# One turn of values moved two products on, spare raw rows and VectorE halves for the first weights, queries and keys stored with their halves side by side

## The chip, the cores and the metric

The kernel runs on one core of a Trainium2 chip. Five engines of that core matter here: TensorE (PE in the profile, with PEld for its weight loads), VectorE (DVE), ScalarE (ACT), GpSimd (POOL) and SyncE (SP), whose queue issues all DMA transfers of this kernel. The metric is the device time of one execution in microseconds (us), as a median of several runs; lower is better.

## The reference

One layer of a hybrid decoder on 2048 tokens of 1024 channels, all in float32:

```python
a = _rmsnorm(h, g_pre_mix[l])
u = jnp.einsum("bsd,dc->bsc", a, w_in[l])          # value | gate | q | k | v, 512 columns each
conv_out = _conformer_conv(c_val, c_gate, ...)     # value * sigmoid(gate), 31 taps, LayerNorm, silu
attn_out = _stick_breaking(q, k, v)                # 8 heads of 64, causal, no softmax
attn_out = _rmsnorm(attn_out, attn_norm_g[l])
y = jnp.einsum("bsc,cd->bsd", concat(conv_out, attn_out), w_out[l])
h = h + _rmsnorm(y, g_post_mix[l])
f_in = _rmsnorm(h, g_pre_ffn[l])
f = jnp.einsum("bsf,fd->bsd", silu(f_in @ w_gate[l]) * (f_in @ w_up[l]), w_down[l])   # 2816 wide
h = h + _rmsnorm(f, g_post_ffn[l])
```

In the stick-breaking attention a query reads only earlier keys, with weight sigmoid(z) times the product of (1 - sigmoid(z)) of all keys between.

## The kernel before

**Precision.** Every float32 operand of a product is split into a rounded half H and a rest L, and a product is made of three passes: L·H, H·H and H·L (`dense`, L606 to L615). A weight's H is a ScalarE copy (L565), its L a GpSimd subtraction (L569) that is also written to DRAM (L571), so that later groups load it (L567) and subtract nothing. `load_w` (L557) does this for one weight tile of 128x1024; its raw rows have two buffers, H and L three each, and `Weights` (L585) loads two products ahead.

**Groups.** The 2048 tokens go in four groups of 512 (`g` from 0 to 3). For each group `inproj` (L766) makes 20 products of 24 matmuls each, four times in the order gate, value ("val"), query, key, value of the attention ("v"), one for each block of 128 columns. Each product fills one PSUM bank of the pool `mm`, which has two banks, taken in turn (`bank`, L527); a product can start only when the engine that reads the bank's product of two turns ago has read it. What reads it: ScalarE's sigmoid for the gate (`sg`, L781), VectorE's multiplication for the value (`glu`, L786), ScalarE and VectorE for the halves of query and key (`split`, L601), ScalarE's copy for v (`vs`, L789).

**The turn of values.** Attention reads differences of neighbouring v rows, transposed. GpSimd makes the differences (`step`, L792 to L794). TensorE transposes them into a bank of the same pool (`vps`, four transposes, L799), and ScalarE and VectorE split that in two parts (`vt`, L804), which SP stores (L805). This is the function `later`; it is called after the next product, the gate of the next block (L776). At the last block of a group it follows at the end.

**Queries and keys in DRAM.** A query or key product holds two heads of 64 rows. Its H and L are stored as four pieces of 64x512 (128 KB each, L817 and L818), by head and half. When a head of a group begins (`begin`, L897), its queries are loaded four times 64x512 into QH and QL, each half of the rows twice; `fetch` (L906) loads one 128x512 piece of keys, H over L.

**Order.** `inproj`, the attention (`attn`), the 31 taps of the convolution (`taps`, VectorE, L833 and L837) and the sums of the feed-forward weights (`sums`, GpSimd, L1201) are recorded one beside the other. Then a planner (`Graph`, L243) takes all recorded instructions, models their durations (`cost`), the waits between them and the DMAs, and fixes the order on each engine by list scheduling with backward priorities in several rounds (`arrange`, L456; `in_order`, L469). It takes overlaps of tiles from `box` (L162). An engine then executes its instructions in that order, so that an instruction that waits holds up all behind it. SP's queue too is in that order, and the built program makes nearly every DMA wait until the one eight places ahead of it has landed. From some 1100 us on the feed-forward products run, to the end.

Of the kernel before, what the change touches and what calls it, by code (L numbers as in the profile page):

```python
# [10 lines left out]
F32 = mybir.dt.float32  # L11
F32R = mybir.dt.float32r
BF16 = mybir.dt.bfloat16
AF = mybir.ActivationFunctionType
ALU = mybir.AluOpType
# [4 lines left out]
P = 128  # L20
S = 2048
D = 1024
# [139 lines left out]
def box(a):  # L162
# [7 lines left out]
    p0, f0 = divmod(int(a.bass_ap.offset), row // size)  # L170
    cur = [(f0, f0 + 1)]
# [9 lines left out]
    return p0, p0 + dims[0][1], [(x * size, y * size) for x, y in cur]  # L181
# [311 lines left out]
def layer_kernel(ctx: ExitStack, tc: tile.TileContext, x, xT, g_pre_mix, w_in, conv_w, conv_b, ln_g, ln_b,  # L493
# [62 lines left out]

    def load_w(w):  # L557
# [5 lines left out]
        raw = wp.tile([P, D], F32, tag="raw", name="raw")  # L563
# [5 lines left out]
        nc.gpsimd.tensor_tensor(L, raw, H.bitcast(F32), ALU.subtract)  # L569
# [98 lines left out]
    for g in range(NG):  # L668
        for h in range(NH):
            qd[h, g] = dp.tile([2, DH, G], F32R, name=f"qd{h}_{g}")  # L670
            kd[h, g] = dp.tile([P, G], F32R, name=f"kd{h}_{g}")
        for p in range(CB):
            vd[p, g] = dp.tile([P, 2, G], F32R, name=f"vd{p}_{g}")
# [92 lines left out]
    def inproj(g, order):  # L766
# [5 lines left out]
        later = None  # L772
        for kind, c in order:
            ps = bank("inps")
            dense([ps], *wts.next(), aH, aL)
            if later is not None:  # L776
                later()
                later = None
# [8 lines left out]
            elif kind == "v":  # L787
# [8 lines left out]
                def later(c=c, vs=step):  # L796
# [9 lines left out]
                    done.add(("v", g, c))  # L806
            else:
# [3 lines left out]
                for h in range(2):  # L811
                    hp = slice(h * DH, (h + 1) * DH)
                    if kind == "q":
                        dsts = (qd[2 * c + h, g][0], qd[2 * c + h, g][1])
                    else:
                        dsts = (kd[2 * c + h, g][0:DH, :], kd[2 * c + h, g][DH:P, :])
                    nc.sync.dma_start(dsts[0].bitcast(F32), H[hp, :].bitcast(F32))  # L817
                    nc.sync.dma_start(dsts[1].bitcast(F32), L[hp, :].bitcast(F32))  # L818
# [3 lines left out]
        if later is not None:  # L822
            later()
# [68 lines left out]
    def attn(g):  # L892
# [4 lines left out]
        def begin(h):  # L897
            QH = ap.tile([P, G], F32R, tag="QH", name="QH")
            QL = ap.tile([P, G], F32R, tag="QL", name="QL")
            for i in range(2):  # L900
                hp = slice(i * DH, (i + 1) * DH)
                nc.sync.dma_start(QH[hp, :].bitcast(F32), qd[h, g][0].bitcast(F32))
                nc.sync.dma_start(QL[hp, :].bitcast(F32), qd[h, g][1].bitcast(F32))
# [897 lines left out]
```

## Time and profile before

| | us |
|---|---|
| median of three runs | 2370.36 (2368.6 to 2370.89) |
| the profiled execution itself | 2367.53 |
| its span, first to last instruction | 2365.4 |

Busy time of the other engines in the span, from the same page: DVE 1711.8 us (72%), ACT 1179.5 us (50%), POOL 1241.8 us (52%). The DMA queue moves 656.68 MB. The granted TensorE clock is 0.998 of full speed on average.

Of the views that the prediction uses, the **waits** view lists for each engine which instruction it was idle for and by whom it was released (total us, times, longest). The **timeline** lists an engine's instructions: start us, duration us, engine, line, operation, output and inputs, and in brackets the idle time before it. A matmul's duration is modelled and overlaps the next one; the distance of two starts is what a matmul costs. The **windows** view gives busy us (and number) of PE, PEld, DVE, ACT and POOL in stretches of the span, then clock, DMA share and GB/s.

### The profile page before, as it was taken

What the parts mean: (1) busy time and instruction counts of PE and PEld (TensorE: products, weight loads), DVE (VectorE), ACT (ScalarE), POOL (GpSimd) and SP (SyncE); (2) the same over time, 40 slices, a digit from 0 to 9 for tenths busy, and PEclk for the clock granted to TensorE, in tenths of its full rate; (3) what the DMA queues carried; (4) which work ended last, traced back from release to release, by engine and by line L of the source; (5) the groups of instructions that cost most, each with busy time, mean ns of one, the idle gap of its engine ahead of it and who ended that gap; (6) DMA issues with size and microseconds to landing.
All of it is one profiled execution on the core that took longest, in us unless ns stands there. A gap on an engine that the chain in (4) does not pass through costs nothing.

```text
span 2365.4 us, 33884 instructions
## 1 busy us (share of the span) xinstructions
PE 2330.6 (99%) x11156; PEld 1927.4 (81%) x11156; DVE 1711.8 (72%) x2121; ACT 1179.5 (50%) x2102; POOL 1241.8 (52%) x1050
## 2 busy tenths in 40 slices
PE   7999999999999999999999999999999999999998
PEld 5878888788888878888888888888888888888886
DVE  5896899899997799946741257888666664557556
ACT  5456555574664455455654554334223335455543
POOL 5473346621652333446510158769976445478556
PEclk9999999999999999999999999999999999999999
DMA  9988877998789799987899768999998667668665
GB/s 329 294 274 309 260 261 236 314 300 266 248 306 301 263 321 321 338 282 269 272 320 318 262 229 308 302 313 332 362 345 291 200 236 232 196 199 297 226 194 178
DMA packets 283791, 656.68 MB, mean 278 GB/s; under 512 B 34912, under 2 KB 35424, under 8 KB 283616
## 3 DMA queue, kind: packets, MB, share of 16 engines
q1 hardware_dynamic: 283616, 654.52, 81.8%
q8 instruction: 88, 1.44, 0.2%
q14 instruction: 87, 0.71, 0.1%
HBM read 460.40 MB, written 193.99 MB: 277 GB/s over the span
## 4 chain that ended last, share of the span: by engine, by line
PE 91%; DVE 4%; DMA 2%; POOL 1%; issue 1%; ACT 1%; SPq 1%; POOLq 0%; DVEq 0%; ACTq 0%
PE b L1117 22%; PE dps L1117 17%; PE c L1117 10%; PE inps L611 5%; PE inps L613 5%; PE inps L615 5%; PE at L946 4%; PE p L1117 3%; PE ops L1053 2%; PE ops L1054 2%; PE ops L1055 2%; PE z L921 2%; PE z L920 2%; PE o L951 2%; PE o L952 2%
## 5 line engine op out<-in xcount | busy, mean ns | idle before, releaser
L837 DVE SCALAR_TENSOR_TENSOR cv<-glu,cw,cv 128x512 f32<-128x512 f32 x464 | 348.0, 750 | 9.0
L1407 POOL TENSOR_TENSOR wL<-raw,wH 128x512 fp32r<-128x512 f32 x176 | 266.4, 1538 | 147.4 <-ACT wH L1406 136.2
L1637 DVE TENSOR_TENSOR xL__20102<-t__20104,xH__20101 128x512 fp32r<-128x512 f32 x154 | 200.0, 1300 | 160.5 <-ACT xH__20101 L1636 156.0
L1635 POOL TENSOR_TENSOR xL__20100<-t__20103,xH__20099 128x512 fp32r<-128x512 f32 x154 | 208.0, 1353 | 157.7 <-ACT xH__20099 L1634 149.3
L604 DVE TENSOR_TENSOR TL<-at,TH 128x512 fp32r<-128x512 f32 (+1 forms) x320 | 189.8, 601 | 125.2 <-ACT TH L603 112.4
L611 PE MATMUL inps<-xH,wL 128*128 128x512 f32 x640 | 257.5, 403 | 7.6 <-ACT sg L781 6.5
L613 PE MATMUL inps<-xH,wH 128*128 128x512 f32 x640 | 255.0, 399 | 0.0
L615 PE MATMUL inps<-xL,wH 128*128 128x512 f32 x640 | 254.4, 399 | 0.0
L928 DVE TENSOR_TENSOR_SCAN om<-z,om,one 128x512 f32<-128x512 f32 x168 | 213.5, 1276 | 45.5 <-ACT z L923 45.0
L1117 PE MATMUL dps<-xH__20099,xL__20102 128*128 128x512 f32 x616 | 239.8, 389 | 0.2 <-DVE xL__20102 L1637 0.2
L1117 PE MATMUL dps<-xH__20099,xH__20101 128*128 128x512 f32 x616 | 239.5, 389 | 0.0
L1117 PE MATMUL dps<-xL__20100,xH__20101 128*128 128x512 f32 x616 | 239.1, 389 | 0.0
L565 ACT ACTIVATE wH<-raw 128x1024 fp32r<-128x1024 f32 x156 | 165.2, 1060 | 144.1 <-PE inps L615 87.7
L923 ACT ACTIVATE z<-z 128x512 f32<-128x512 f32 (+2 forms) x320 | 167.2, 528 | 97.6 <-PE z L921 92.8
L603 ACT ACTIVATE TH<-at 128x512 fp32r<-128x512 f32 (+1 forms) x320 | 169.1, 534 | 82.0 <-PE at L946 70.9
L569 POOL TENSOR_TENSOR wL<-raw,wH 128x1024 fp32r<-128x1024 f32 x50 | 120.6, 2413 | 151.3 <-ACT wH L565 103.2
L1634 ACT ACTIVATE xH__20099<-t__20103 128x512 fp32r<-128x512 f32 x154 | 97.2, 631 | 205.5 <-POOL xL__20100 L1635 165.6
L946 PE MATMUL at<-idr,om 128*128 128x128 f32 x1088 | 185.5, 272 | 0.6 <-DVE om L928 0.4
L1406 ACT ACTIVATE wH<-raw 128x512 fp32r<-128x512 f32 x176 | 101.6, 624 | 167.8 <-PE b L1117 65.5
L946 PEld LDWEIGHTS at<-idr,om 128*128 128x128 f32 x1088 | 137.8, 140 | 37.3 <-DVE om L928 1.6
L1201 POOL TENSOR_TENSOR sum<-sum 128x512 f32<-128x512 f32 x88 | 117.5, 1335 | 66.3 <-issue 22.1
L611 PEld LDWEIGHTS inps<-xH,wL 128*128 128x128 f32 x640 | 121.0, 189 | 30.8 <-ACT sg L781 7.6
(295 smaller groups left out, 6029.8 us busy)
## 6 DMA issues: line engine op xcount, KB each, us to landing
wL<-wL SPq DMA_DIRECT2D x156, 512.0 KB, 5.3
raw<-in_w_in_dram SPq DMA_DIRECT2D x80, 512.0 KB, 5.7
t__20104<-u SPq DMA_DIRECT2D x154, 256.0 KB, 3.0
c<-c SPq DMA_DIRECT2D x88, 256.0 KB, 4.9
t__20103<-wd SPq DMA_DIRECT2D x88, 256.0 KB, 2.7
K<-kd SPq DMA_DIRECT2D x80, 256.0 KB, 4.5
V<-vd SPq DMA_DIRECT2D x80, 256.0 KB, 4.6
u<-accf SPq DMA_DIRECT2D x22, 768.0 KB, 6.7
```

What stands on the lines that cost most here:

```text
L603: nc.scalar.activation(H, ps, AF.Copy)
L604: nc.vector.tensor_tensor(L, ps, H.bitcast(F32), ALU.subtract)
L611: nc.tensor.matmul(ps, WL[:, kc], aH[t](k), start=k == 0, stop=False)
L613: nc.tensor.matmul(ps, WH[:, kc], aH[t](k), start=False, stop=False)
L615: nc.tensor.matmul(ps, WH[:, kc], aL[t](k), start=False, stop=k == KT - 1)
L837: nc.vector.scalar_tensor_tensor(to, gl[c][:, k:k + G], cw[:, c, k:k + 1], a, ALU.mult, ALU.add)
L928: nc.vector.tensor_tensor_scan(r, zr, one.to_broadcast([P, w]), hd_["prev"][j], ALU.mult, ALU.bypass)
L946: nc.tensor.transpose(pt[:, j * P:(j + 1) * P], u["A"][j][:, b * P:(b + 1) * P], id32)
L1117: return nc.tensor.matmul(ps, a, b, skip_group_check=True, **flags)
L1407: nc.gpsimd.tensor_tensor(l, t, f32(h), sub)
L1635: nc.gpsimd.tensor_tensor(WL, w, f32(WH), sub)
L1637: nc.vector.tensor_tensor(UL, t, f32(UH), sub)
```

## The change

Five edits:

1. `later` becomes `turn` and waits in a list; the turn of v runs after the second product behind it (value of the next block), not the first (gate).
2. Every second weight tile of the first group takes its raw rows from a new tile `raw2` (`spare`), made in the buffers that the mixed outputs use later; so up to four raw tiles more can be in flight.
3. The L halves of the first four weight tiles are subtracted by VectorE, not GpSimd.
4. Queries and keys lie in DRAM as 128 x 2 x 512, H and L of a row side by side. A product is stored by two transfers of 128x512 (256 KB), not four of 64x512; a head's queries are loaded by two transfers of 64x1024, not four of 64x512, with the two copies on every other partition. That makes 64 stores and 64 loads less. A key tile then holds H and L in alternate rows, as the query tile holds its two copies.
5. `box` is told how to cover steps between partitions and rows that are part of a DRAM row.

```diff
+    halves_ = []
+
+    def spare():
+
+        if not halves_:
+            t = cm.tile([P, 2, D], F32, tag="big", name="raw2", bufs=2)
+            halves_.extend([t[:, 1, :], t[:, 0, :]])
+        return halves_.pop()
...
-        raw = wp.tile([P, D], F32, tag="raw", name="raw")
+        raw = spare() if src is w_in and key not in kept and len(kept) % 2 else wp.tile([P, D], F32, tag="raw", name="raw")
...
-        nc.gpsimd.tensor_tensor(L, raw, H.bitcast(F32), ALU.subtract)
+        (nc.vector if len(kept) < 4 else nc.gpsimd).tensor_tensor(L, raw, H.bitcast(F32), ALU.subtract)
...
-        for h in range(NH):
-            qd[h, g] = dp.tile([2, DH, G], F32R, name=f"qd{h}_{g}")
-            kd[h, g] = dp.tile([P, G], F32R, name=f"kd{h}_{g}")
         for p in range(CB):
+            qd[p, g] = dp.tile([P, 2, G], F32R, name=f"qd{p}_{g}")
+            kd[p, g] = dp.tile([P, 2, G], F32R, name=f"kd{p}_{g}")
...
-        later = None
-        for kind, c in order:
+        behind = []
+        for n, (kind, c) in enumerate(order):
             ps = bank("inps")
             dense([ps], *wts.next(), aH, aL)
-            if later is not None:
-                later()
-                later = None
+            if behind and behind[0][0] <= n:
+                behind.pop(0)[1]()
...
-                def later(c=c, vs=step):
+                def turn(c=c, vs=step):
...
+                behind.append((n + 2, turn))
...
-                for h in range(2):
-                    hp = slice(h * DH, (h + 1) * DH)
...
-                    nc.sync.dma_start(dsts[0].bitcast(F32), H[hp, :].bitcast(F32))
-                    nc.sync.dma_start(dsts[1].bitcast(F32), L[hp, :].bitcast(F32))
+                to = (qd if kind == "q" else kd)[c, g]
+                for a, t in enumerate((H, L)):
+                    nc.sync.dma_start(to[:, a, :].bitcast(F32), t.bitcast(F32))
...
-            QH = ap.tile([P, G], F32R, tag="QH", name="QH")
-            QL = ap.tile([P, G], F32R, tag="QL", name="QL")
+            Q = ap.tile([P, 2, G], F32R, tag="Q", name="Q")
+            half = qd[h // 2, g][h % 2 * DH:(h % 2 + 1) * DH]
             for i in range(2):
-                hp = slice(i * DH, (i + 1) * DH)
-                nc.sync.dma_start(QH[hp, :].bitcast(F32), qd[h, g][0].bitcast(F32))
-                nc.sync.dma_start(QL[hp, :].bitcast(F32), qd[h, g][1].bitcast(F32))
+                nc.sync.dma_start(Q[slice(i, P, 2), :, :].bitcast(F32), half.bitcast(F32))
...
-            nc.sync.dma_start(K.bitcast(F32), kd[h, c].bitcast(F32))
+            half = kd[h // 2, c][h % 2 * DH:(h % 2 + 1) * DH].rearrange("p a t -> (p a) t")
+            nc.sync.dma_start(K.bitcast(F32), half.bitcast(F32))
```

Because the planner orders everything anew, instructions move on all engines. Three places follow, each as the built programs have it (line, operation, output and inputs, shape of the output, and how many in a row).

On ScalarE, around the first turn of the first group: before, from the copy of the first key to the second gate's sigmoid `sg`.

```order
L603 ACTIVATE qkH<-inps 128x512
L724 ACTIVATE xcol<-xcol,gpm 128x512 x6
L789 ACTIVATE vs<-inps 128x512
L724 ACTIVATE xcol<-xcol,gpm 128x512 x2
L565 ACTIVATE wH<-raw 128x1024 x2
L603 ACTIVATE vt<-vps 128x4x64 x2
L781 ACTIVATE sg<-inps 128x512
```

The same stretch of ScalarE in the changed kernel, from the H half of the eighth weight tile on:

```order
L578 ACTIVATE wH<-raw_450 128x1024
L736 ACTIVATE xcol<-xcol,gpm 128x512 x2
L800 ACTIVATE vs<-inps 128x512
L736 ACTIVATE xcol<-xcol,gpm 128x512
L578 ACTIVATE wH<-raw 128x1024
L736 ACTIVATE xcol<-xcol,gpm 128x512
L792 ACTIVATE sg<-inps 128x512
L578 ACTIVATE wH<-raw_741 128x1024
L616 ACTIVATE vt<-vps 128x4x64
L736 ACTIVATE xcol<-xcol,gpm 128x512
L616 ACTIVATE vt<-vps 128x4x64
```

The sigmoid of the second gate stood behind both `vt` copies and now stands ahead of them.

On VectorE at the same place, before: the taps of the first conv block (`cv`, the last one writes `acc`), the query and key halves `qkL`, and the two `vt` parts; the second block's multiplication `glu_140` comes only after nine more rows, of the attention and of the next query product.

```order
L604 TENSOR_TENSOR qkL<-inps,qkH 128x512
L837 SCALAR_TENSOR_TENSOR cv<-glu_138,cw,cv 128x512 x7
L604 TENSOR_TENSOR qkL<-inps,qkH 128x512
L837 SCALAR_TENSOR_TENSOR cv<-glu_138,cw,cv 128x512 x16
L837 SCALAR_TENSOR_TENSOR acc<-glu_138,cw,cv 128x512
L604 TENSOR_TENSOR vt<-vps,vt 128x4x64 x2
```

And in the changed kernel:

```order
L617 TENSOR_TENSOR qkL<-inps,qkH 128x512
L845 SCALAR_TENSOR_TENSOR cv<-glu_138,cw,cv 128x512 x7
L617 TENSOR_TENSOR qkL<-inps,qkH 128x512
L845 SCALAR_TENSOR_TENSOR cv<-glu_138,cw,cv 128x512 x15
L845 SCALAR_TENSOR_TENSOR acc<-glu_138,cw,cv 128x512
L797 TENSOR_TENSOR glu_140<-inps,sg 128x512
L841 TENSOR_SCALAR cv<-glu_140,cw,small_121 128x512
L617 TENSOR_TENSOR vt<-vps,vt 128x4x64
L845 SCALAR_TENSOR_TENSOR cv<-glu_140,cw,cv 128x512 x2
L617 TENSOR_TENSOR vt<-vps,vt 128x4x64
```

The second block's multiplication now follows the last tap directly, ahead of both `vt` parts.

On VectorE at the start of the program, before: the scaled token rows `xrow`, the halves `xL` of the first group's input, the first multiplication and the first taps.

```order
L648 CAST idr<-ident 128x128
L697 TENSOR_SCALAR xrow<-xrow,rs 128x1024 x4
L624 SCALAR_TENSOR_TENSOR xL<-tps,gpm,xH 128x512 x8
L786 TENSOR_TENSOR glu_138<-inps,sg 128x512
L833 TENSOR_SCALAR cv<-glu_138,cw,small_121 128x512
```

And in the changed kernel:

```order
L661 CAST idr<-ident 128x128
L709 TENSOR_SCALAR xrow<-xrow,rs 128x1024 x3
L582 TENSOR_TENSOR wL<-raw,wH 128x1024
L709 TENSOR_SCALAR xrow<-xrow,rs 128x1024
L582 TENSOR_TENSOR wL<-raw_311,wH 128x1024
L582 TENSOR_TENSOR wL<-raw,wH 128x1024
L637 SCALAR_TENSOR_TENSOR xL<-tps,gpm,xH 128x512 x8
L582 TENSOR_TENSOR wL<-raw_311,wH 128x1024
L797 TENSOR_TENSOR glu_138<-inps,sg 128x512
```

One of the four weight halves stands ahead of the fourth token row, two ahead of all `xL`, and one behind them. ScalarE likewise makes three weight copies `wH`, where it made two, ahead of its eight `xH`.

More of the change, by code (lines that the diff above doesn't have):

```diff
@@ L170, in box @@
     p0, f0 = divmod(int(a.bass_ap.offset), row // size)
+    step, rows = dims[0]
+    if step * size % row:
+        return p0, p0 + -(-step * size * rows // row) + (f0 > 0), [(0, row)]
+    rows = (rows - 1) * (step * size // row) + 1
     cur = [(f0, f0 + 1)]
@@ L180, in box @@
             cur = [(x + step * k, y + step * k) for k in range(n) for x, y in low]
-    return p0, p0 + dims[0][1], [(x * size, y * size) for x, y in cur]
+    return p0, p0 + rows, [(x * size, y * size) for x, y in cur]
 def meet(a, b):
@@ L810, in inproj @@
                 split(ps, H, L)
-                for h in range(2):
-                    hp = slice(h * DH, (h + 1) * DH)
[L813 to L816, printed above, removed]
-                    nc.sync.dma_start(dsts[0].bitcast(F32), H[hp, :].bitcast(F32))
-                    nc.sync.dma_start(dsts[1].bitcast(F32), L[hp, :].bitcast(F32))
+                to = (qd if kind == "q" else kd)[c, g]
+                for a, t in enumerate((H, L)):
+                    nc.sync.dma_start(to[:, a, :].bitcast(F32), t.bitcast(F32))
             if kind != "v":
@@ L821, in inproj @@
             yield 1
-        if later is not None:
-            later()
+        for _, turn in behind:
+            turn()
     conv = {}
@@ L897, in begin @@
         def begin(h):
-            QH = ap.tile([P, G], F32R, tag="QH", name="QH")
-            QL = ap.tile([P, G], F32R, tag="QL", name="QL")
+            Q = ap.tile([P, 2, G], F32R, tag="Q", name="Q")
+            half = qd[h // 2, g][h % 2 * DH:(h % 2 + 1) * DH]
             for i in range(2):
-                hp = slice(i * DH, (i + 1) * DH)
-                nc.sync.dma_start(QH[hp, :].bitcast(F32), qd[h, g][0].bitcast(F32))
-                nc.sync.dma_start(QL[hp, :].bitcast(F32), qd[h, g][1].bitcast(F32))
-            return dict(QH=QH, QL=QL, prev=[lower[:, 0:1]] * TT, o=None)
+                nc.sync.dma_start(Q[slice(i, P, 2), :, :].bitcast(F32), half.bitcast(F32))
+            return dict(Q=Q, prev=[lower[:, 0:1]] * TT, o=None)
         def fetch(h, c):
@@ L919, in scores @@
             js = slice(j * P, (j + 1) * P)
-            nc.tensor.matmul(z[:, 0:w], hd_["QL"][:, js], K[:, 0:w], start=True, stop=False)
-            nc.tensor.matmul(z[:, 0:w], hd_["QH"][:, js], K[:, 0:w], start=False, stop=True)
+            nc.tensor.matmul(z[:, 0:w], hd_["Q"][:, 1, js], K[:, 0:w], start=True, stop=False)
+            nc.tensor.matmul(z[:, 0:w], hd_["Q"][:, 0, js], K[:, 0:w], start=False, stop=True)
             om = ap.tile([P, G], F32, tag="om", name="om", bufs=NOM)
```

## The prediction

> **What bounds the kernel now.** I read the page's busy times first, then TensorE's own waits, then the windows by stage, then the timeline where a wait is long.
>
> ```profile
> span 2365.4 us, 33884 instructions
> PE 2330.6 (99%) x11156; PEld 1927.4 (81%) x11156; DVE 1711.8 (72%) x2121; ACT 1179.5 (50%) x2102; POOL 1241.8 (52%) x1050
> ...
> PE tps L621 <- DVE xrow L697: 8.9, 4, 7.2
> PE inps L611 <- ACT sg L781: 6.5, 4, 4.1
> PE po L984 <- DVE ot L976: 3.7, 2, 2.8
> ...
> PE inps L611 <- POOL wL L569: 1.1, 1, 1.1
> ...
> 50.00:60.00 10.00, 4.80 (x18) 3.41 (x17) 6.48 (x10) 2.31 (x4) 5.12 (x6) 0.83 1.01 320
> 60.00:200.00 140.00, 136.76 (x710) 114.67 (x709) 128.71 (x192) 72.85 (x140) 78.81 (x71) 1.00 0.90 299
> 200.00:1100.00 900.00, 893.75 (x4576) 738.75 (x4575) 775.72 (x1055) 510.92 (x915) 380.31 (x371) 1.00 0.84 284
> 1100.00:2300.00 1200.00, 1199.91 (x5448) 992.97 (x5447) 729.28 (x782) 537.54 (x950) 703.34 (x521) 1.00 0.81 273
> ```
>
> TensorE is busy 99% of the span, and from 1100 to 2300 us it idles 0.09 us in 1200 (1200.00 - 1199.91). The change takes no matmul away, so it can win only what TensorE waits for before 1100 us: 5.2 us between 50 and 60 us, 3.24 (140.00 - 136.76) and 6.25 (900.00 - 893.75) after that, and something of the start, whose 8.9 us are mostly the wait for the first tokens. No line of TensorE's waits names a DMA. The one large piece is at 51 us.
>
> ```profile
> 51.02 0.39 PE L615 MATMUL inps<-xL,wH 128*128 128x512 f32 x1
> 52.46 0.66 PE L799 MATMUL vps<-idr,step 128*128 128x128 f32 x4 [1.05 <-POOL step L793]
> 57.26 0.80 PE L611 MATMUL inps<-xH,wL 128*128 128x512 f32 x1 [4.14 <-ACT sg L781]
> 57.85 0.63 PE L613 MATMUL inps<-xH,wH 128*128 128x512 f32 x1
> 58.28 0.63 PE L615 MATMUL inps<-xL,wH 128*128 128x512 f32 x1
> ...
> 60.27 0.40 PE L613 MATMUL inps<-xH,wH 128*128 128x512 f32 x1
> 60.50 0.40 PE L615 MATMUL inps<-xL,wH 128*128 128x512 f32 x1
> ...
> 90.11 0.60 PE L799 MATMUL vps<-idr,step 128*128 128x128 f32 x4
> 90.47 0.49 PE L615 MATMUL inps<-xL,wH 128*128 128x512 f32 x1
> ...
> 48.85 2.41 POOL L569 TENSOR_TENSOR wL<-raw,wH 128x1024 fp32r<-128x1024 f32 x1 [6.07 <-ACT wH L565]
> 51.20 1.05 POOL L792 TENSOR_TENSOR step<-vs 128x511 f32<-128x511 f32 x1
> ...
> 53.15 0.38 ACT L603 ACTIVATE vt<-vps 128x256 fp32r<-128x256 f32 x1 [0.87 <-PE vps L799]
> 56.33 0.38 ACT L603 ACTIVATE vt<-vps 128x256 fp32r<-128x256 f32 x1 [2.80 <-DVE vt L604]
> 56.61 0.59 ACT L781 ACTIVATE sg<-inps 128x512 f32<-128x512 f32 x1
> ...
> 29.75 0.69 DVE L786 TENSOR_TENSOR glu<-inps,sg 128x512 f32<-128x512 f32 x1 [8.39 <-PE inps L615]
> ...
> 42.56 12.62 DVE L837 SCALAR_TENSOR_TENSOR cv<-glu,cw,cv 128x512 f32<-128x512 f32 x16
> 55.22 0.75 DVE L837 SCALAR_TENSOR_TENSOR acc<-glu,cw,cv 128x512 f32<-128x512 f32 x1
> 55.88 0.42 DVE L604 TENSOR_TENSOR vt<-vps,vt 128x256 fp32r<-128x256 f32 x1
> ```
>
> It is a chain through three engines. GpSimd makes `step` only at 51.20, behind a weight half; so the transposes start at 52.46. VectorE is in the middle of 16 taps and takes the first `vt` at 55.88. ScalarE's second `vt` waits for that, and the sigmoid `sg` stands behind it; the next product needs the bank that `sg` reads. Without the waits the transposes would start 0.23 us after 51.02 (the distance of 60.27 and 60.50), and the product 0.36 us later (four transposes at full rate, 90.11 to 90.47), at 51.61. From 57.26 until 60.27 seven matmuls are issued, at half rate (58.28 is 0.43 after 57.85); at 0.23 they would end at 51.61 + 1.61 = 53.2. TensorE is back at full rate at 60.27, so this turn costs **7.1 us** (60.27 - 53.2): 5.2 of waiting, the rest of half rate after it.
>
> **The change part by part.** *The first turn.* In the changed order the value product of the second block follows the gate at once: its bank is the one that `vs` read long before. It ends 24 steps later, at 51.25 + 24 x 0.23 = 56.8, and only then come the transposes. `step` now stands behind the weight half of the eighth tile, which ScalarE copies ahead of `vs`: the product of v ends at 45.8 (51.25 less one product of 5.5), the copy takes 1.06 (row at 11.75, below), the half 2.41 and `step` 1.05 with two short parts, so it is made by about 51, over 5 us ahead of need. `sg` stands ahead of `vt`, so nothing of the turn holds it. That removes the 7.1. What is late next is the multiplication of the value product: after four transposes the query product needs the value's bank. VectorE has ended its last tap at 55.97 (55.22 + 0.75) and is free, so `glu` runs from 56.8 to 57.5 (0.69, row at 29.75) against transposes that end at 57.15: **0.4 us** of new wait. Queued behind `glu` are the next block's first taps and the `vt` parts, some 3 us, and the key product that needs their bank starts only at 63.
>
> *The start.* The first five rows are the timeline before; the last three are groups that give prices.
>
> ```profile
> 11.75 1.06 ACT L565 ACTIVATE wH<-raw 128x1024 fp32r<-128x1024 f32 x1 [0.24 <-DMA raw<-in_w_in_dram]
> 12.79 2.42 ACT L623 ACTIVATE xH<-tps,gpm 128x512 fp32r<-128x512 f32 x4
> ...
> 11.47 0.75 DVE L697 TENSOR_SCALAR xrow<-xrow,rs 128x1024 f32<-128x1024 f32 x1 [0.71 <-POOL rs L547]
> ...
> 14.49 0.79 PE L611 MATMUL inps<-xH,wL 128*128 128x512 f32 x1 [1.09 <-POOL wL L569]
> ...
> 19.60 0.48 PE L615 MATMUL inps<-xL,wH 128*128 128x512 f32 x1
> ...
> L569 POOL TENSOR_TENSOR wL<-raw,wH 128x1024 fp32r<-128x1024 f32 x50 | 120.6, 2413 | 151.3 <-ACT wH L565 103.2
> ...
> L1165 DVE TENSOR_TENSOR xL<-sumin,xH 128x512 fp32r<-128x512 f32 x4 | 2.5, 678 | 0.0
> ...
> L1414 DVE TENSOR_TENSOR a<-glu,a 128x512 f32<-128x512 f32 x7 | 10.1, 1436 | 0.1
> ```
>
> GpSimd's 2.41 us per half is no longer what the first product waits for (1.09 of TensorE's idle time). A half on VectorE is not in the trace. Two VectorE subtractions of half the width cost 2 x 0.678 = 1.36 where both operands come from SBUF and nothing disturbs, and 2 x 1.436 = 2.87 in the slowest such group; I take 1.36, since GpSimd has only short work then, and keep the other end for the range. The gain is spent again: the fourth token row stands behind one half (+1.36 against its start at 11.47), and ScalarE makes a third weight copy (1.06) before its first `xH` at 12.79, once that weight has landed. So `xH` begins about 14.2, the first matmul about 14.9, not 14.49. Two halves more (2.7 us) delay the first `xL`, and the last transposes with it; but the changed order puts five matmuls, not three, ahead of them, so that behind the last transposes 17 of the product are left, where before 19 were left at 19.60. I take **+0.5 us**; at best -1 (the matmuls in hand weigh more), at worst +3.
>
> The weights behind these four keep GpSimd, and with spare rows they land earlier. Since the H and L tiles still number three, a copy cannot run before the product three back has ended; the rows therefore save nothing on TensorE where no product waits for a weight, as after 14.49 none does. I cost them at 0; the cover is a product of 5.5 us.
>
> *Half as many transfers.* SP issues 128 fewer.
>
> ```profile
> K<-kd SPq DMA_DIRECT2D x80, 256.0 KB, 4.5
> ...
> QH<-qd SPq DMA_DIRECT2D x64, 128.0 KB, 4.4
> ```
>
> A 256 KB transfer lands in 4.5 us and a 128 KB one in 4.4, so half the places in the queue come free. As TensorE waits for no DMA, this is 0 on its path, with a gain of up to 2 us through other engines (bound below). A destination of every other partition is not in the trace: it may land like the 256 KB row, 4.5 us, or as two such, 9; I take 4.5, the same size, and on TensorE's path 0 either way by the same cover.
>
> *The other turns.* Fifteen remain; four stand at a group's end, as before. At the eleven others the gate's sigmoid had caused 6.5 - 4.1 = 2.4 us more. In the new order it has a whole product's time. In exchange the query product needs `glu` at once, which before had a whole product's time. I take this exchange as even: 0; its bounds are -2.4 and rival 1.
>
> **Sum:** -7.1 + 0.4 + 0.5 = -6.2 us. The span becomes 2359.2. The profiled execution took 2367.53 with a span of 2365.4, and the median lies 2.83 above it; so 2370.36 - 6.2 = **2364.2 us**.
>
> *Two rules of the Trainium skill.* The spacing of 0.43 us after the long wait against 0.23 (rows at 57.85 and 60.27) is the clock. TensorE: Matmul & The Clock Gate, What's actually happening, says that an idle window of about 3.4 us halves the clock and a busy one of that length restores it. The trace agrees: 4.14 us of idle time, then 3.0 us at half rate. By it the new wait of 0.4 us costs no clock, and a start with sparser matmuls could stay cold longer, which is the third case below. SBUF — State Buffer, SBUF: two separate sides, says that a VectorE instruction with two SBUF inputs and a GpSimd one that reads SBUF lock each other out for a whole instruction. The two groups of 0.678 and 1.436 us above fit that. By it the halves on VectorE would cost 2.87 each beside GpSimd sums, and the start +3, not +0.5.
>
> **The rivals.**
>
> 1. *The multiplication takes the sigmoid's place as a wait (slower).*
>
> ```profile
> L928 DVE TENSOR_TENSOR_SCAN om<-z,om,one 128x512 f32<-128x512 f32 x168 | 213.5, 1276 | 45.5 <-ACT z L923 45.0
> L786 DVE TENSOR_TENSOR glu<-inps,sg 128x512 f32<-128x512 f32 x16 | 11.0, 684 | 15.5 <-PE inps L615 15.3
> ```
>
> After the first turn VectorE is the fuller engine: 775.72 of 900 us, ScalarE 510.92. At the eleven turns the query product follows the value product after other TensorE work that comes to 0.9 to 2.6 us, mostly about 1.2 (as many transposes and matmuls as the changed order has there, at 0.09 and 0.23 each). If a scan (1.28) has just begun, `glu` ends 1.28 + 0.68 = 1.96 later: 0.76 too late. With a tap (0.75) besides it is 1.5. Eleven times 0.76 is 8.4; with the sigmoid's 2.4 gone, -6.2 - 2.4 + 8.4 = -0.2, or 2370. Eleven times 1.5 is 16.5: +7.9, or **2378**. It decides from 0.8 us a turn. Against it: `sg` had the same tight place before, and only four of sixteen waited. Chance 0.22, of which 0.12 above 2375.
>
> 2. *More waits go than the first turn's.* `po` 3.7, `sg` 2.4, and the rest of the 9.5 us of idle time in 60 to 1100 us depend on the order; with transfers earlier, half may go: -6.2 - 4.7, or 2359.5. Chance 0.13.
>
> 3. *A colder start.* The 17 matmuls left run at 0.43, not 0.23: 3.4 us instead of 0.5, so 2370.4 - 7.1 + 0.4 + 3.4 = 2367. Chance 0.1.
>
> 4. *The change doesn't do what it says:* the value's bank or `step` is late by as much, since taps fill VectorE from 29.75 on, and the stall only moves: 2370. The tap chain's end at 55.97 against 56.8 speaks against it, by 0.8 us only. Chance 0.05.
>
> **How the numbers follow.** The forecast has 0.5, with 2359 to 2369 as its own range, since waits of 9.5 us are dealt anew. About 0.2% (4.7 us) is what a measurement of this kernel can tell from no change. Faster than 2365.6: 0.42 of the forecast's 0.5 and the 0.13, together 0.55. Within: 0.08, 0.1 of rival 1, 0.1 and 0.05, together 0.33. Slower than 2375.1: 0.12. The range from 2356 to 2373 leaves out rival 1's upper part and a little below.
>
> **What would show it.** Right: no TensorE idle time over 1 us between 20 and 60 us, `sg` gone from TensorE's waits or under 1 us, a wait of the first query product for `glu` under 1 us, the clock at full rate from 25 us on, 1100 us to the end unchanged. Wrong: `inps <- DVE glu` with more than 7 us in all, a first product that ends 2 us later than before, or a `po` wait grown by several us.

## The result, and the profile after

| | before | changed |
|---|---|---|
| median, us | 2369.48 (4 runs, 2368.59 to 2370.89) | 2353.58 (4 runs, 2352.93 to 2354.17) |
| span of the profiled execution, us | 2365.4 | 2351.1 |

The ratio is 0.9933, with a 95% interval of 0.992 to 0.9947: 15.9 us faster. The forecast was 6.2 us, with a range whose lower end (2356) lies 2.4 us above the result. The direction and the first turn came as forecast; more than half of the gain came from elsewhere. One execution of the last run below (e18) took 4061.07 us at a granted clock of 0.642, in a slow state, and is left out of its median.

The page of the changed kernel, its span and busy times, then TensorE's waits (us in all, times, longest), then four windows (busy us and number of PE, PEld, DVE, ACT, POOL, then clock, DMA share, GB/s):

```profile
span 2351.1 us, 33675 instructions
PE 2328.0 (99%) x11156; PEld 1926.8 (82%) x11156; DVE 1720.7 (73%) x2125; ACT 1176.6 (50%) x2102; POOL 1228.2 (52%) x1046
```

```profile
PE tps L634 <- DVE xrow L709: 9.3, 4, 7.3
PE o L958 <- ACT TH L616: 0.8, 2, 0.6
PE z L927 <- DVE om L935: 0.8, 2, 0.5
...
PE inps L624 <- DVE glu L797: 0.4, 1, 0.4
```

```profile
50.00:60.00 10.00, 9.58 (x44) 7.74 (x44) 8.72 (x14) 5.10 (x8) 5.03 (x3) 1.00 0.98 353
60.00:200.00 140.00, 138.92 (x724) 116.34 (x724) 126.43 (x193) 75.91 (x146) 83.74 (x79) 1.00 0.91 317
200.00:1100.00 900.00, 898.03 (x4604) 744.32 (x4603) 787.15 (x1058) 515.35 (x929) 398.06 (x391) 1.00 0.85 291
1100.00:2300.00 1200.00, 1199.79 (x5434) 992.40 (x5433) 728.41 (x776) 531.21 (x937) 683.62 (x499) 1.00 0.79 266
```

TensorE's busy time hardly moved (2330.6 to 2328.0); what went is idle time. Between 50 and 60 us it fell from 5.20 to 0.42 us, between 60 and 200 from 3.24 to 1.08, between 200 and 1100 from 6.25 to 1.97. The waits for `sg` (6.5), `po` (3.7) and `step` (1.5, the row of the kernel before below) are gone, and `glu` stands there with 0.4 in all.

```profile
PE vps L799 <- POOL step L793: 1.5, 2, 1.1
```

The timeline of the changed kernel at the first turn, on the four engines:

```profile
48.16 1.04 POOL L803 TENSOR_TENSOR step<-vs 128x511 f32<-128x511 f32 x1
...
51.66 0.58 ACT L792 ACTIVATE sg<-inps 128x512 f32<-128x512 f32 x1
...
56.49 0.37 ACT L616 ACTIVATE vt<-vps 128x256 fp32r<-128x256 f32 x1
...
53.80 0.75 DVE L845 SCALAR_TENSOR_TENSOR acc<-glu,cw,cv 128x512 f32<-128x512 f32 x1
55.55 0.69 DVE L797 TENSOR_TENSOR glu<-inps,sg 128x512 f32<-128x512 f32 x1 [0.99 <-PE inps L628]
...
55.28 0.60 PE L810 MATMUL vps<-idr,step 128*128 128x128 f32 x4
56.29 0.50 PE L624 MATMUL inps<-xH,wL 128*128 128x512 f32 x1 [0.42 <-DVE glu L797]
```

`step` and the short parts behind it are made over 5 us ahead of the transposes, `sg` starts 4.8 us ahead of the first `vt`, and VectorE has ended its last tap and even waits 0.99 us for the product of the value. The query product starts with a wait of 0.42 us, and the clock stays at full speed (1.00 in the window, 0.83 before).

And the start of the changed kernel, ScalarE, VectorE and TensorE:

```profile
9.64 1.06 ACT L578 ACTIVATE wH<-raw 128x1024 fp32r<-128x1024 f32 x1
...
12.23 1.06 ACT L578 ACTIVATE wH<-raw 128x1024 fp32r<-128x1024 f32 x1 [0.28 <-DMA raw<-in_w_in_dram]
13.20 2.42 ACT L636 ACTIVATE xH<-tps,gpm 128x512 fp32r<-128x512 f32 x4
...
10.73 1.22 DVE L582 TENSOR_TENSOR wL<-raw,wH 128x1024 fp32r<-128x1024 f32 x1 [0.57 <-ACT wH L578]
11.88 0.74 DVE L709 TENSOR_SCALAR xrow<-xrow,rs 128x1024 f32<-128x1024 f32 x1
12.54 2.35 DVE L582 TENSOR_TENSOR wL<-raw,wH 128x1024 fp32r<-128x1024 f32 x2
14.81 2.72 DVE L637 SCALAR_TENSOR_TENSOR xL<-tps,gpm,xH 128x512 fp32r<-128x512 f32 x4
...
13.93 0.80 PE L624 MATMUL inps<-xH,wL 128*128 128x512 f32 x1
...
18.30 0.60 PE L634 MATMUL tps<-idr,xrow 128*128 128x128 f32 x4
18.66 0.47 PE L628 MATMUL inps<-xL,wH 128*128 128x512 f32 x1
```

A half on VectorE takes 1.22 us. The first `xH` starts at 13.20 and the first product at 13.93, 0.56 us earlier than before (14.49), not 0.4 later. The sixth product (the second block's gate, 24 matmuls ahead of the value product that ends at 55.28) ends at 55.28 - 24 x 0.227 = 49.83, where it ended at 51.25: the start won 1.4 us.

### The profile page after: what moved, and what is told of

The parts are those of the page before. It is cut to its first block, busy times and chain, and to the rows that moved or that the text cites. A ratio compares the mean times of both kernels' runs of the same rounds, so it can differ in the third digit from the quotient of the medians.

```text
span 2351.1 us, 33675 instructions
## 1 busy us (share of the span) xinstructions
PE 2328.0 (99%) x11156; PEld 1926.8 (82%) x11156; DVE 1720.7 (73%) x2125; ACT 1176.6 (50%) x2102; POOL 1228.2 (52%) x1046
## 4 chain that ended last, share of the span: by engine, by line
PE 96%; DVE 2%; POOL 1%; issue 1%; DMA 0%; ACT 0%; SPq 0%; POOLq 0%; DVEq 0%
PE b L1124 21%; PE dps L1124 17%; PE c L1124 10%; PE inps L624 6%; PE inps L628 6%; PE inps L626 6%; PE at L953 5%; PE z L928 3%; PE o L958 3%; PE o L959 3%; PE z L927 3%; PE p L1124 3%; PE ops L1060 3%; PE ops L1062 3%; PE ops L1061 2%; PE pf L974 1%
## 5 line engine op out<-in xcount | busy, mean ns | idle before, releaser
L582 POOL TENSOR_TENSOR wL<-raw,wH 128x1024 fp32r<-128x1024 f32 x46 | 110.5, 2402 | 149.0 <-ACT wH L578 122.2
L1124 PE MATMUL c<-xH,wL 128*128 128x512 f32 x352 | 140.8, 401 | 0.1
```

The lines of the kernel that those rows point to most:

```text
L1124: return nc.tensor.matmul(ps, a, b, skip_group_check=True, **flags)
```

## The experiments

Each edit was made alone, each was undone in the changed kernel, and some kernels got another order from the planner without any other edit. One table holds all runs. "Gaps" are worked out from the trace of each run: the distance from one matmul's start to the next, less the usual one (0.227 us for 512 columns, 0.17 for 384, 0.114 for 256, 0.11 for 128), added up where it is over 0.15 us. Such gaps make 26.8 us before and 12.9 after, and their difference is nearly all of the 14.3 us between the spans. The ratio is against the kernel before, run beside each on the same chip; gains against it are told by the ratio (0.001 is 2.4 us), differences between two changed kernels by their medians. The kernel before ran at 2369.48 us beside the changed kernel and at up to 2370.9 beside the others, so differences against the changed kernel can be up to some 1.8 us smaller by the ratios; both are given where that matters.

| kernel | median, us | ratio (95%) | gaps to 46 us | 46 to 66 | 66 to 1100 | after |
|---|---|---|---|---|---|---|
| before | 2369.5 to 2370.9 | 1 | 6.1 | 6.9 | 13.2 | 0.6 |
| changed | 2353.58 | 0.9933 (0.992 to 0.9947) | 5.2 | 0.6 | 6.0 | 1.1 |
| e1 turn alone | 2365.23 | 0.9979 (0.997 to 0.9988) | 5.9 | 5.2 | 12.1 | 0.8 |
| e2 rows and halves alone | 2368.24 | 0.9999 (0.999 to 1.0008) | 5.4 | 6.4 | 13.2 | 1.5 |
| e3 layout alone | 2363.7 | 0.9977 (0.9968 to 0.9986) | 5.7 | 2.5 | 11.7 | 0.8 |
| e4 before, other order | 2367.0 | 0.9989 (0.9981 to 0.9998) | 6.0 | 5.6 | 13.0 | 0.4 |
| e5 changed, no turn | 2360.78 | 0.9959 (0.9947 to 0.9972) | 5.0 | 4.6 | 9.6 | 0.8 |
| e6 changed, no layout | 2361.92 | 0.9964 (0.9951 to 0.9978) | 5.3 | 0.6 | 11.3 | 3.8 |
| e7 changed, no rows or halves | 2356.1 | 0.9936 (0.9924 to 0.9949) | 6.5 | 0.7 | 6.8 | 1.3 |
| e8 changed, other order | 2354.06 | 0.993 (0.9918 to 0.9943) | 5.5 | 0.6 | 7.9 | 0.4 |
| e9 changed, all transfers cut | 2358.0 | 0.9948 (0.9934 to 0.9961) | 5.0 | 0.9 | 7.9 | 0.9 |
| e10 stores cut | 2353.05 | 0.9928 (0.9915 to 0.994) | 5.5 | 0.6 | 5.6 | 0.6 |
| e11 loads cut | 2354.53 | 0.9933 (0.992 to 0.9945) | 5.6 | 0.6 | 6.7 | 1.5 |
| e12 no layout, other order | 2360.22 | 0.9955 (0.9943 to 0.9968) | 5.5 | 0.6 | 11.3 | 1.5 |
| e13 no layout, new `box` | 2357.51 | 0.9946 (0.9933 to 0.9958) | 6.0 | 0.3 | 10.6 | 1.6 |
| e14 before, new `box` | 2366.39 | 0.9984 (0.9975 to 0.9993) | 6.3 | 5.1 | 12.8 | 0.6 |
| e15 all cut, other order | 2353.86 | 0.9929 (0.9916 to 0.9941) | 5.5 | 0.0 | 7.4 | 0.4 |
| e16 turn three products later | 2355.49 | 0.9936 (0.9924 to 0.9949) | 5.3 | 0.0 | 9.5 | 1.2 |
| e17 no layout, `ot` on ScalarE | 2356.54 | 0.9945 (0.9932 to 0.9958) | 5.8 | 0.3 | 8.5 | 1.6 |
| e18 changed, `ot` on ScalarE | 2356.6 | 0.9946 (0.9933 to 0.9959) | 5.8 | 0.6 | 8.2 | 1.8 |

### Each part alone, and another order

e1 makes edit 1 alone, e2 edits 2 and 3, e3 edits 4 and 5; e4 gives the planner another number:

```diff
-HOP = 60.0
+HOP = 61.0
```

> The kernel before with the turn two products later alone; raw rows, halves and DRAM layout as before. Four theories of the 15.9 us (2369.5 to 2353.6). A, the turn: it takes the first stall of 7.1 us and also the later waits of the products for sg and of the transposes for step (some 4 us of TensorE idle time between 60 and 1100 us); then this kernel gains 10 to 14 us, and sg and step are gone from TensorE's waits. B, GpSimd and the raw rows: the turn gains the 7.1 only if step is ready in time, and step still stands behind GpSimd's halves; gain 3 to 7 us, with a wait for step or sg left between 50 and 60 us. C, the transfers: gain about 6.5 us (the first stall less the new wait), the waits after 60 us stay near the 9.5 us in all that they were. D, the planner's new order by chance: gain 6.5 plus or minus what the unrelated order changes give, with waits after 60 us of other kinds than before.

> The kernel before with the spare raw rows and VectorE's halves of the first four weight tiles alone; the turn follows the next product as before. A, the turn: nothing but the earlier start, 1 to 2 us; the stall at 51 us (sg 4.1 us) stays, as vt still waits for VectorE's taps and sg for vt. B, GpSimd and the raw rows: step is made some 2.4 us or more earlier, the stall at 51 us shrinks from 5.2 to under 2 us, and waits for step and for the first weights go: gain 5 to 9 us. C, the transfers: as A. D, chance: 1 to 2 us from the start, plus or minus 3 us from waits after 60 us.

> The kernel before with queries and keys side by side in DRAM and half as many transfers alone; turn, raw rows and halves as before. A and B: within 2 us of before, the stall at 51 us as it was, the idle time of TensorE between 60 and 1100 us still about 9.5 us. C, the transfers: the waits for po (3.7 us) and part of the others between 60 and 1100 us go, so a gain of 4 to 8 us, with the stall at 51 us still there. D, chance: plus or minus 3 us, by waits that are neither of transfers nor of the layout.

> The kernel before with one number of the planner's model (HOP, what it takes a signal between engines to cost) 61 instead of 60 ns: the same instructions, only dealt in another order. A, B and C: within 2 us of before, the same stall at 51 us. D, chance: the waits after 60 us (9.5 us of TensorE's idle time) come out otherwise, by 3 us or more, without any edit to the program; then what one order and another differ by is of the size of the gain that was not forecast, about 9 us.

The turn alone won 5 us, not 10 to 14: `sg` was gone, but the stall had moved. TensorE's timeline and VectorE's in that kernel:

```profile
34.26 0.69 DVE L604 TENSOR_TENSOR qkL<-inps,qkH 128x512 fp32r<-128x512 f32 x1 [12.75 <-ACT qkH L603]
35.45 0.69 DVE L785 TENSOR_TENSOR glu<-inps,sg 128x512 f32<-128x512 f32 x1 [0.49 <-PE inps L615]
...
43.04 17.37 DVE L838 SCALAR_TENSOR_TENSOR cv<-glu,cw,cv 128x512 f32<-128x512 f32 x22
60.32 0.69 DVE L785 TENSOR_TENSOR glu<-inps,sg 128x512 f32<-128x512 f32 x1
...
57.26 0.60 PE L798 MATMUL vps<-idr,step 128*128 128x128 f32 x4
61.15 0.71 PE L611 MATMUL inps<-xH,wL 128*128 128x512 f32 x1 [3.29 <-DVE glu L785]
```

In this kernel the planner had the first value product run in turns with the query product. It ended at about 35.4 us, where the changed kernel's `glu` starts at 28.34, so VectorE's taps ran on until 60.3, ahead of the second block's `glu`, and the query product waited 3.3 us for `glu`. That is the fourth rival of the prediction, in another kernel than the one it was made for: the margin of 0.8 us to the end of the taps is real, and one order keeps it while another doesn't.

Rows and halves alone won nothing that can be told from noise (the interval reaches 0.1% below and above 1; by the medians they won 1.9 us); TensorE's wait there is the old one:

```profile
PE inps L620 <- ACT sg L790: 9.5, 7, 4.6
```

The layout alone won 5.5 us, most of it at the first turn (gaps of 6.9 to 2.5), though it does not touch the turn. In its order `step` is made at 46.32, ahead of the weight half that it stood behind before, and what ends last is that half:

```profile
46.32 1.04 POOL L803 TENSOR_TENSOR step<-vs 128x511 f32<-128x511 f32 x1 [3.91 <-ACT vs L800]
...
51.44 2.35 POOL L582 TENSOR_TENSOR wL<-raw,wH 128x1024 fp32r<-128x1024 f32 x1 [3.68 <-ACT wH L578]
...
53.85 0.50 PE L624 MATMUL inps<-xH,wL 128*128 128x512 f32 x1 [2.32 <-POOL wL L582]
```

The same program in another order (e4) won 2.6 us. So a difference of 2 to 3 us between two such kernels can be the order alone.

### Each part undone

e5 puts `behind.append((n + 1, turn))` for `n + 2`; e6 has the layout of before, e7 `raw` and GpSimd's halves of before; e8 is the changed kernel with HOP 61.

> The changed kernel with the turn back behind the next product; spare rows, VectorE's halves and the DRAM layout stay. The runs so far: the turn alone gained 4.9 us, halves and rows alone 1.9 at most, the layout alone 6.5, and another order of the kernel before alone 3.2. A, the turn is what the others lean on: the chain of vt and sg at the first turn comes back, with a wait for sg of 4 us or more between 50 and 60 us, and the time is 6 to 9 us above the changed kernel (2360 to 2363). C, the transfers carry it: 2 us above it, about 2356, and no wait for sg over 1 us. D, chance: the first turn stalls for something else (as in the layout alone, for a weight's half, 2.5 us), and the waits after 60 us come to anything from 3 to 10 us: 2356 to 2364.

> The changed kernel with queries and keys in DRAM as before, in four pieces; the turn, the spare rows and VectorE's halves stay. A: the first turn costs under 1 us and the time stays within 3 us of the changed kernel (2354 to 2357). C, the transfers: the 6.5 us of the layout alone are lost, 2360, with waits for po and others back between 60 and 1100 us (9 us of TensorE's idle time, not 3.3). D, chance: first turn under 1 us as the same edits stand around it, and waits after 60 us of 4 to 9 us: 2355 to 2360.

> The changed kernel without spare raw rows and with GpSimd's halves for all first weights; the turn and the layout stay. In the turn alone the value product of the first block ran interleaved with the query product and ended at 35.4 us, so VectorE's 31 taps ended at 60.3 and the multiplication behind them held the next product for 3.3 us. B, the halves and rows decide that: the first glu is again at about 35 us, the wait for glu 3 us, and the start 1.4 us later: 2357 to 2359. C and A: the first glu at about 29 us, no such wait, only the start is later: 2355. D, chance: 2355 to 2361, by waits after 60 us.

> The changed kernel with the same one number of the planner (HOP) 61 instead of 60 ns: the same instructions in another order. A, B and C: within 2 us of the changed kernel, as the edits' effects do not hang on one order. D, chance: the changed kernel holds a lucky order of the waits after 60 us (3.3 us of idle time, against 9.5 before), and another order gives some of it back: 3 to 7 us slower than the changed kernel, 2357 to 2361, though still 6 us or more faster than before.

Without the turn 7.2 us are lost (2353.58 to 2360.78), and the wait is the one that the prediction followed:

```profile
PE inps L624 <- ACT sg L792: 3.8, 3, 3.1
```

Without the layout 8.3 us are lost, without rows and halves 2.5, not more than an order is worth. By the ratios the three come to 6.2, 7.3 and 0.7 us. The one other order of the changed kernel that was run came out the same (2354.06), so nothing speaks for a lucky order. Turn and layout together are the gain (e7: 0.9936), and each is worth more beside the other than alone.

### What of the layout counts

e9 to e11 keep the new layout and cut its transfers in two again, e10 the stores and e11 the loads alone:

```diff
-                    nc.sync.dma_start(to[:, a, :].bitcast(F32), t.bitcast(F32))
+                    for r in (slice(0, DH), slice(DH, P)):
+                        nc.sync.dma_start(to[r, a, :].bitcast(F32), t[r, :].bitcast(F32))
...
-                nc.sync.dma_start(Q[slice(i, P, 2), :, :].bitcast(F32), half.bitcast(F32))
+                for a in range(2):
+                    nc.sync.dma_start(Q[slice(i, P, 2), a, :].bitcast(F32), half[:, a, :].bitcast(F32))
```

e12 is e6 and e15 is e9 with HOP 61; e13 is e6 and e14 the kernel before with the new `box`; e16 is the changed kernel with `n + 3`.

> The changed kernel, all edits kept, with halves side by side, but its transfers cut in two again: each store of 128x512 as two of 64x512, each load of 64x1024 as two of 64x512, so that SP issues as many as before. The layout's edit is worth 8.3 us (2361.9 without it, 2353.6 with it). N, the number of transfers is what counts, since each holds one of SP's eight places: the time goes back to 2359 to 2362, and the waits after 60 us that stand in the run without the layout (11.3 us of gaps between matmuls up to 1100 us, 6.0 in the changed kernel) are back. S, the layout itself counts (one query tile, one wait, keys of both halves in alternate rows): within 2 us of the changed kernel. D, chance in the planner's order: anything between, 2354 to 2362.

> The changed kernel with only the stores of queries and keys cut in two again (64 transfers more, 128 KB each; the loads stay whole). N, by the number alone: half of what the transfers are worth is lost, 2357 to 2358; if the stores are what matters, since they come in the same stretch as the input weights, all of it, 2360 to 2362, and the run with cut loads loses nothing. S: within 2 us of the changed kernel. D: 2354 to 2360 without a relation to the run with cut loads.

> The changed kernel with only the loads of queries cut in two again (64 transfers more of 128 KB; the stores stay whole). N, by the number alone: 2357 to 2358; if the loads are what matters, since attention waits for them, 2360 to 2362, and the run with cut stores loses nothing. S: within 2 us of the changed kernel. D: 2354 to 2360 without a relation to the run with cut stores.

> The kernel without the layout (turn, spare rows and halves kept, queries and keys in four pieces) in another order of the planner (HOP 61). In its own order it took 2361.9, and 7.6 us of its gaps stood at four places: po at 155 us 4.3, o at 1114 us 1.2, c at 1248 us 1.6, po at 115 us 0.6. N and S, the layout's edit is worth its 8 us in any order: 2360 to 2363. D, those places are chance: another order removes some of them, and the time comes to 2355 to 2359, near the changed kernel.

> The kernel without the layout (turn, spare rows and halves kept, queries and keys in four pieces), but with the new box, which alone differs from the run without the layout (2361.9; 2360.2 in another order). The old box took the H and the L piece of a head's queries in DRAM (rows 0 to 63 and 1 to 64 of its count) for overlapping, so that the planner held each load of queries back behind both stores; the new one does not. X, the cover counts: with it the planner's order is as good as in the changed kernel, 2353 to 2356, and the waits between 60 and 1100 us fall from 11.3 to about 6 us of gaps. N, the number of transfers counts (3.6 us by the run with all transfers cut): 2358 to 2362, no better than without. D, chance: 2357 to 2362, by waits at other places.

> The kernel before with the new box alone: the same instructions and transfers, and only what the planner takes to overlap differs. The layout's whole edit alone took 5.5 us off (2363.7). X, the cover counts: 2363 to 2366. N: 2368 to 2372, as before. D, chance: 2365 to 2371; another order of the kernel before took 2.6 us off.

> The changed kernel with all its transfers of queries and keys cut in two, as in the run that took 2358.0, in another order of the planner (HOP 61). N, the number of transfers counts: 2357 to 2360 again. D, chance: with cut stores alone and cut loads alone the time stayed at 2353.1 and 2354.5, so the 4 us may be that one order; another comes to 2353 to 2356.

> The changed kernel with the turn one product later still (behind the third product, the query of the next block). In the changed kernel the wait for glu at the first turn is 0.4 us, as the query product needs the value's bank right behind the transposes. A, more room: the wait for glu goes (0.6 us of gap at the first turn), other turns gain at most 1 us: 2352 to 2354. D, chance: 2352 to 2358 by other waits; attention gets its values 5.5 us later at each turn, so a wait of TensorE at a group's start of 3 us or more would speak against it.

The number of transfers is not it: stores alone and loads alone cost nothing, and all of them cost 4.4 us in one order and nothing in another (2358.0, 2353.86). The forecast of 0 for the queue itself holds. Without the layout another order stays at 2360.2, so its worth does not hang on that one order. The new `box` alone took 3.8 us off the kernel before and 4.4 off the kernel without the layout. It changes only what the planner holds to overlap, but that is another order too, and of the size that orders have differed by here (2.6, 0.5, 1.7 and 4.1 us in four pairs); two gains alike speak for it and do not settle it. One product more for the turn (e16) took the wait for `glu` away and won nothing: 2355.49, where more room alone had been given 2352 to 2354; the gaps after 66 us grew from 6.0 to 9.5.

What the kernels with the turn and without the layout have in common stands at `po`, the transposes behind a pair of heads. The changed kernel without the layout (e6), VectorE, GpSimd and TensorE at 150 us:

```profile
149.12 6.20 DVE L986 TENSOR_TENSOR ot<-ot,ss 128x512 f32<-128x512 f32 x1
...
148.57 1.28 POOL L1034 TENSOR_TENSOR oT<-oT,vsh 64x512 f32<-64x512 f32 x1
149.82 4.95 POOL L761 TENSOR_TENSOR xL<-xcol,xH 128x512 fp32r<-128x512 f32 x4
...
155.37 0.66 PE L994 MATMUL po<-idr,ot 128*128 128x128 f32 x4 [4.11 <-DVE ot L986]
```

The multiplication of `ot` takes 0.68 us on its own. Here it starts while GpSimd is at work, and ends only when five GpSimd instructions in a row are through; TensorE waits 4.11 us. The kernel before has the same at 121 us, where GpSimd's row is `oT`, a weight half and `step` (VectorE, GpSimd, TensorE):

```profile
121.11 5.08 DVE L976 TENSOR_TENSOR ot<-ot,ss 128x512 f32<-128x512 f32 x1
...
121.04 1.29 POOL L1024 TENSOR_TENSOR oT<-oT,vsh 64x512 f32<-64x512 f32 x1 [0.49 <-ACT oT L1016]
122.29 2.35 POOL L569 TENSOR_TENSOR wL<-raw,wH 128x1024 fp32r<-128x1024 f32 x1
124.61 1.03 POOL L792 TENSOR_TENSOR step<-vs 128x511 f32<-128x511 f32 x1
...
126.24 0.66 PE L984 MATMUL po<-idr,ot 128*128 128x128 f32 x4 [2.83 <-DVE ot L976]
```

And the same multiplication in the changed kernel, then the taps and GpSimd's `xL` behind it:

```profile
145.93 0.68 DVE L983 TENSOR_TENSOR ot<-ot,ss 128x512 f32<-128x512 f32 x1
...
149.37 3.91 DVE L845 SCALAR_TENSOR_TENSOR cv<-glu,cw,cv 128x512 f32<-128x512 f32 x5
...
149.43 3.77 POOL L764 TENSOR_TENSOR xL<-xcol,xH 128x512 fp32r<-128x512 f32 x3 [0.44 <-ACT xH L763]
```

It is through before GpSimd's row begins, and what stands beside that row are taps, which lose nothing (3.91 / 5 = 0.78 each). In all four kernels with the turn, without the layout and with `ot` on VectorE (e1, e6, e12, e13) one `ot` took 5.1 to 6.2 us and `po` waited 2.4 to 4.6 us in all; in the changed kernel and those with turn and layout none took over 2.7. (The layout alone had one of 5.2 that TensorE did not wait for.) Where turn and layout are both missing the hold comes and goes with the order: 5.1 us in the kernel before, none over 2.4 and no wait for `po` in e2 and e4, and in e14 a wait of 2.8 us for `po` with no `ot` over 2.8.

The planner does reckon with such a hold: in `forward` (L421 of the kernel before) an instruction of VectorE or GpSimd that `in_sbuf` (L231) marks waits for the one in hand and is next in turn. In that model `ot` loses the rest of one GpSimd instruction at most; a hold through five of them has no price in it, so an order can run into one or miss it without the planner knowing.

The last two runs took that instruction off VectorE:

```diff
-                nc.vector.tensor_tensor(o3, o3, ss[:, 1, :].unsqueeze(2).to_broadcast([P, 2 * TT, DH]), ALU.mult)
+                for k in range(2 * TT):
+                    nc.scalar.activation(o3[:, k, :], o3[:, k, :], AF.Copy, scale=ss[:, 1, k:k + 1])
```

> The kernel without the layout (2361.9), with one multiplication moved: the head pair's output ot times its ss (a VectorE instruction of 0.68 us on its own) is made on ScalarE, in eight pieces of 128x64. In the run without the layout that instruction started at 149.12 us beside five GpSimd instructions in a row (oT, then four xL) and ended only behind them, 6.20 us later; TensorE's po waited 4.1 us for it. In the changed kernel and its other orders it took 0.68 us at this place. L, the hold by GpSimd is what the layout's edit takes away by moving the two apart: the wait for po at 155 us falls under 1 us and the time to 2357 to 2359. N, it is something else, such as transfers: po waits on, and the time stays at 2360 to 2363. D, chance: po gone, but other waits in its place, 2358 to 2362.

> The changed kernel with the same multiplication on ScalarE in eight pieces. L: there was no wait for po here, so nothing is to be gained: within 2 us of the changed kernel (2352 to 2355); that the run without the layout gains more than this one shows the hold, not the moved work. D, chance: 2351 to 2357 by other waits.

Without the layout it won 5.4 us and `po` waits no more; in the changed kernel it lost 3, more than the account by the hold alone allowed (2352 to 2355), so the moved work or its order has a cost of its own. Both come to the same time, 2356.5 and 2356.6: in this pair, where `ot` can't be held, the layout is worth nothing. It is one pair, and orders alone have differed by up to 4.1 us. Not all of the 5.4 us is the hold: `po` had 4.9 us of gaps, 2.8 us of gaps at 1114 and 1248 us went too, which have no part in it, and new ones of up to 1.2 us came up. No run beat the changed kernel by more than runs differ (e10, 2353.05, is the best).

## Why the prediction was wrong, and where it was right

**First turn, -7.1 and +0.4: right.** The gaps from 46 to 66 us fell by 6.3 (6.9 to 0.6), against 6.7 forecast. Each link came as written: `step` ahead of need, `sg` ahead of `vt`, the new wait for `glu` 0.42 us, no loss of clock. Undoing the turn brings `sg` back. All signs that the prediction gave for being right are there; but beyond `sg` none of them concerns the waits from 60 to 1100 us, and there most of the gain that was not forecast lies. The condition under it (taps that end ahead of the value product) held in the changed kernel, and failed in the turn alone, at 3.3 us.

**The start, +0.5: wrong, in its sign too.** Measured -1.4, outside its own bounds of -1 to +3. The halves cost 1.22 and 2.35 / 2, not 1.36 each, and the last two token rows were squared sooner (the `wH` behind them at 9.64, before at 10.45), which paid for most of ScalarE's third copy: the first `xH` came at 13.20, where 14.2 was forecast. The halves did put off the first `xL` (14.81, before 13.51), but the matmul behind the last transposes started at 18.66, before at 19.60, so that delay did not reach TensorE. There 17 matmuls of the product were left, before 19, as forecast. Undoing rows and halves makes the gaps up to 46 us 1.3 longer (5.2 to 6.5), and alone they made them 0.7 shorter.

**The other turns, "I take this exchange as even: 0": this step failed.** It costed the multiplication at the later turns at as much as the sigmoid had cost. TensorE waits for `sg` in all six kernels with the turn behind the next product (0.5 to 9.5 us in all) and in none of the fourteen with it later, and in those `glu` was waited for 0.0 to 0.8 us, but for the 3.3 of the turn alone. The bound of -2.4 was the right value, and the sum had 0. Rival 1 priced a scan (1.28) in the way of `glu` at each turn; that did not come up.

**Half as many transfers, 0, and no term for `po`: this step failed too, and by more.** The 0 was right about the queue, where cut transfers show nothing, and yet the layout's edit was worth 7.3 to 8.3 us. As far as the runs show, the gain came through the order: in the orders with turn and layout no `ot` was held over 2.7 us. The prediction put the waits for `po` (3.7 us) down to "the order" in rival 2 and left them out of the sum. 2.8 of them are the hold at 126 us, a row of 5.08 us on VectorE for an instruction that takes 0.68; the rest is a wait at 451 us without a hold (`ot` takes 0.69 there). The rule of the Trainium skill on SBUF — State Buffer, SBUF: two separate sides, was weighed in the prediction for the start alone, where GpSimd had little to do, and not for `ot`, which was held here.

**The range.** Rival 2 let half of the 9.5 us of idle time after 60 us go, and put 0.13 on it. 6.4 went (9.49 to 3.05). With the sigmoid's -2.4 and the 3.7 of `po` in the sum, and the start at -1.4, the same working gives -7.1 + 0.4 - 1.4 - 2.4 - 3.7 = -14.2 against 14.3 measured in the spans. The other 1.6 us of the 15.9 lie between span and median: the prediction carried one offset over, but the median lies 4.1 us above the profiled span before (2369.48 and 2365.4) and 2.5 in the changed kernel (2353.58 and 2351.1). Why that offset shrank is not shown.

**What stays open:** how much of the layout's worth is the better cover of overlaps (`box`) and how much the data's new form; how much of it is the hold of `ot`; and why each part is worth more beside the others. The runs show orders that differ by up to 4.1 us for no other reason, and one or two orders of each kernel do not part the two.

## What to carry to other kernels

When an edit goes through a planner, look at each wait of the bounding engine that is left, not at the largest alone, and read the row of the instruction that ended it: a duration several times its usual one names a cause that any new order may take away or bring. Judge an edit by the kernel with all others in it as well as alone; here the three parts won 5.0, 0.2 and 5.5 us alone and 15.9 together. Before a gain of a few us is put down to an edit, run the same program in another order: here that moved the time by 0.5 to 4.1 us.

## What the hardware showed that was not expected

VectorE's instruction with both inputs in SBUF did not get in between GpSimd's instructions: it was held through five of them, 6.20 us for 0.68. The Trainium skill, SBUF — State Buffer, SBUF: two separate sides, has the port held for one whole instruction; the trace shows that the one who waits may not get the next turn. The taps beside the same GpSimd work lost nothing; they read `glu` from SBUF and `cv` from PSUM.

A multiplication by one value per row can be held as well. In the kernel before with another order (e4), VectorE's fourth token row and GpSimd's weight halves:

```profile
11.00 2.83 DVE L697 TENSOR_SCALAR xrow<-xrow,rs 128x1024 f32<-128x1024 f32 x1 [0.72 <-POOL rs L547]
...
10.93 5.11 POOL L569 TENSOR_TENSOR wL<-raw,wH 128x1024 fp32r<-128x1024 f32 x2
```

It took 2.83 us, where the other rows of this kind that are quoted have 0.74 or 0.75, and the first product of that kernel started at 15.22 us (before: 14.49). The Trainium skill, SBUF — State Buffer, Who interferes with whom, counts this operation in its fast modes among those that contend; the row agrees. TensorE's clock went to half after a wait of 3.08 us (e5: its matmuls stand 0.43 us apart from 54.11 us on) and stayed full after one of 2.32 (e3: 0.23 apart). So a wait shorter than the 3.4 us that the prediction quotes already cost clock here.

A load to every other partition, which the prediction could only bound, is among the changed kernel's DMA issues (KB each, median us to landing):

```profile
Q<-qd SPq DMA_DIRECT2D x64, 256.0 KB, 5.5
```

It lands in 5.5 us, near the 4.5 taken and far from 9.
